# A decoder layer with experts: a sorted token list from one-hot products, adds per block, norm passes moved, one branch at the end

## Chip, cores and metric

The kernel runs on one core of a Trainium2 chip. The metric is device time in microseconds (us) of one execution. The median of three runs of the kernel before is 1720.96 us (1716.74 to 1729.13).

## What is computed

One layer of a decoder on 2048 tokens of width 1024, in float32. A mixer (windowed attention, a gated recurrence, attention into memory) and its output projection come first, then a layer norm, then a mixture of 16 experts of which each token takes two, then a second layer norm. The change lies in the expert part and in the second norm. Cut to that, the reference is:

```python
def moe(x, w_router, router_bias, w_gate, w_up, w_down):
    idx, w = route(x2, w_router, router_bias)        # two experts and weights per token
    ...                                              # assignments sorted by expert, in blocks
    def expert_block(args):
        xb, e = args
        h = jax.nn.silu(xb @ w_gate[e]) * (xb @ w_up[e])   # 1024 -> 512
        return h @ w_down[e]                                # 512 -> 1024
    ys = lax.map(expert_block, (xs, block_expert)).reshape(cap, D)
    y = jnp.zeros((n_tok, D), x.dtype).at[slot_tok].add(ys * slot_w[:, None])
    return y.reshape(B, S, D)

x = layer_norm(ALPHA * x + mix @ w_out[l], ln1_g[l], ln1_b[l])
x = layer_norm(ALPHA * x + moe(x, ...), ln2_g[l], ln2_b[l])
```

## The kernel before

The expert part begins at about 960 us of the span. `plan_slots` orders the experts by load into 16 slots s = 0 to 15, and slot s has a capacity of CAPS[s] rows, from 336 down to 256. For each slot the kernel runs `gemm1` (rows times gate and up weights, in four column blocks j; products of high and low parts, so 192 matmuls), which leaves h in a high and a low part (`L1599`, `L1600`, and `L1602` for the rows beyond a full block), and then `gemm2` (h times the down weights, by blocks of at most 128 rows, 12 matmuls for each half of the columns). The transposes of the next slot's rows (`L1484` on TensorE, `L1486` on ScalarE and VectorE) are interleaved with `gemm2`. Weights arrive over SyncE's queue, a SyncE transfer for each; ScalarE makes the high part (`L1583`, `L1560`) and VectorE the low part (`L1584`, `L1561`). `fetch` loads a small table of a slot's token numbers and weights (`tab`, also SyncE's queue), VectorE turns it into indices (`L1463`), and POOL gathers the rows of x1 (`L1471`).

Each block's result z goes to DRAM with an indirect DMA that adds into c.z (`L1673`, POOL). The DRAM tensor is one object to the dependency tracker, so each such add waits for the one before to land. c.z starts as the output of the first norm.

Tokens whose two slots are both done can have their second norm while later slots run. For that `plan_order` sorts all tokens by the later of their two slots, in six steps (`next(order_)`), spread over s = 3 to 7. It computes each token's place in the list on VectorE and scatters the token numbers to their places in DRAM, 16 indirect DMAs on POOL (`L1343`) in s = 6, and loads the list back (`L1347`) in s = 7. READY says how many blocks of 128 tokens of this list are complete after each slot: 2, 3, 5, 6, 8, 10, 12 after s = 7 to 13; the last four are taken up after s = 14. From s = 8 on `bring` gathers such blocks from c.z (`L1524`, POOL; three buffers, tile zt) and in the following slot `norm` does them: `scale` (statistics `L1531`, `L1533`, `L1535` on VectorE, a power on POOL, `L1536`) and `write` (two passes over 1024 columns, `L1541` and `L1542`, on VectorE, and an indirect write to the output, `L1546`, on POOL). With `issue_after` the VectorE work of block n is put behind the multiply of column block n (scale) and n + 1 (write) of `gemm1`, at most the fourth. In the last slot these four follow, and its own two blocks get their norm in `gemm2` itself (`normed`, `L1501` to `L1515`, with 832 columns on VectorE and the rest on ScalarE and POOL; writes `L1678`).

TensorE's order is that of the program text. The other engines' orders come from a scheduler that lays the instructions out with estimated times when the kernel is built. At the end stand two loops whose number of turns is read at run time: the first (`L1754`) does blocks over capacity, the second (`L1762`) norms all rows again where the list was not ready. With these inputs both have zero turns. `If` and loop blocks are scheduled as a unit on all engines.

## Time and profile before

| | us |
|---|---|
| median of 3 runs | 1720.96 |
| the profiled execution's own time | 1723.19 |
| its span, first to last instruction | 1721.7 |
| TensorE busy | 1544.5 (90%) |
| VectorE busy | 1199.9 (70%) |
| ScalarE busy | 755.7 (44%) |
| POOL busy | 600.5 (35%) |
| mean granted TensorE clock | 0.957 of full |
| moved by DMA | 260.77 MB, 151 GB/s over the span |

A share of busy time is an average over stages that have different limits. For the expert part one reads the windows from slot to slot: how long each is, how much of it TensorE is busy, and which wait stands in what is left. Idle time of an engine that is not the bound costs nothing. A wait for several semaphores is put down to the one that came last by the profile; where the engine named had long been done, it was another, often a DMA.

### The profile page before, as it was taken

How to read it: one execution, taken by the hardware profiler on the slowest of the kernel's cores; microseconds unless marked ns; L12 is line 12 of the kernel's file. 1: busy time of each engine (PE TensorE's matmuls, PEld its weight loads, DVE VectorE, ACT ScalarE, POOL GpSimd, SP SyncE). 2: the span in 40 equal slices, each digit the busy share in tenths (PEclk: the TensorE clock that was granted, in tenths of full speed). 3: DMA queues.
4: the chain of work that ended last, by engine and by line, in shares of the span. 5: the costliest groups of instructions: out<-in, count | busy, mean ns of one | idle time of the engine just before them, and what ended most of it. 6: DMA issues, size and time to landing. Idle time of an engine off the chain costs nothing. (4 is left out here: it accounts for less than half of the span.)

```text
span 1721.7 us, 28673 instructions
## 1 busy us (share of the span) xinstructions
PE 1544.5 (90%) x10277; PEld 1377.6 (80%) x10277; DVE 1199.9 (70%) x2900; ACT 755.7 (44%) x1589; POOL 600.5 (35%) x798
## 2 busy tenths in 40 slices
PE   8899999878899989879999599999999889998991
PEld 7899999877888888667777489998887778888881
DVE  5688888994988888768888546655555445665664
ACT  4566676764122212233332344555554445444430
POOL 3233333465554554322332222111123323242243
PEclk9999999998999999889999799999999999999996
DMA  9422222342122112263441598777767668898853
GB/s 275 140 93 93 93 93 93 129 129 82 50 63 69 56 55 93 71 223 114 158 159 74 181 266 206 203 202 199 198 185 175 168 177 231 246 271 228 236 163 117
DMA packets 241166, 260.77 MB, mean 151 GB/s; under 512 B 25301, under 2 KB 190358, under 8 KB 241020
## 3 DMA queue, kind: packets, MB, share of 16 engines
q1 hardware_dynamic: 213680, 182.11, 34.6%
q0 software_dynamic: 22224, 71.84, 15.7%
q10 hardware_dynamic: 5116, 4.94, 0.9%
q8 instruction: 83, 1.36, 0.3%
q14 instruction: 63, 0.52, 0.1%
HBM read 189.97 MB, written 70.60 MB: 151 GB/s over the span
## 5 line engine op out<-in xcount | busy, mean ns | idle before, releaser
L62 PE MATMUL ph<-xt,w 128*128 128x256 f32 (+8 forms) x3072 | 402.0, 292 | 10.0 <-ACT w L1583 3.8
L62 PEld LDWEIGHTS ph<-xt,w 128*128 128x128 f32 x3072 | 398.7, 190 | 14.7 <-DVE w L1584 5.0
L62 PE MATMUL pj<-xt,w 128*128 128x256 f32 x2016 | 293.8, 290 | 13.1 <-DVE xt L138 3.9
L62 PEld LDWEIGHTS pj<-xt,w 128*128 128x128 f32 x2016 | 262.6, 193 | 19.4 <-DVE xt L138 5.3
L1636 PE MATMUL py<-w,h 128*128 128x512 f32 (+8 forms) x936 | 253.1, 416 | 23.4 <-DVE h L1600 17.7
L1636 PEld LDWEIGHTS py<-w,h 128*128 128x128 f32 (+8 forms) x936 | 165.7, 185 | 72.7 <-DVE h L1600 21.6
L1584 DVE TENSOR_TENSOR w<-raw,w 128x1024 fp32r<-128x1024 f32 x128 | 153.7, 1218 | 67.8 <-ACT w L1583 67.6
L62 PE MATMUL py<-w,xt 128*128 128x512 f32 x672 | 172.7, 405 | 0.0
L1583 ACT ACTIVATE w<-raw 128x1024 fp32r<-128x1024 f32 x128 | 132.6, 1054 | 60.4 <-PE ph L62 34.0
L1673 POOL DMA_INDIRECT zd<-z,io x40 | 65.9, 1646 | 262.6 <-ACT xt L1486 147.0
L62 PEld LDWEIGHTS py<-w,xt 128*128 128x128 f32 x672 | 123.0, 191 | 27.1 <-issue 4.6
L1486 DVE TENSOR_TENSOR xt<-tr,xt 128x512 fp32r<-128x512 f32 (+8 forms) x84 | 49.4, 595 | 71.2 <-ACT xt L1486 71.0
L62 PE MATMUL pj<-w,xt 128*128 128x512 f32 x336 | 89.3, 405 | 0.0
L793 DVE TENSOR_TENSOR qb<-qq,F 64x256 f32<-64x256 f32 x112 | 83.4, 745 | 2.0
L338 POOL TENSOR_SCALAR prob<-prob,den 128x128 f32<-128x128 f32 x128 | 45.8, 376 | 107.7 <-ACT prob L381 57.8
L1486 ACT ACTIVATE xt<-tr 128x512 fp32r<-128x512 f32 (+8 forms) x84 | 43.7, 520 | 74.4 <-PE tr L1484 74.4
L1471 POOL DMA_INDIRECT xg<-x1d,ig x42 | 45.0, 1072 | 86.9 <-ACT w L1560 31.5
L811 DVE COPY_PREDICATED A<-mask,pl 128x512 f32<-128x512 uint8 x56 | 50.1, 894 | 34.5 <-PE pl L809 33.6
L1561 DVE TENSOR_TENSOR w<-raw,w 128x2048 fp32r<-128x2048 f32 x32 | 73.1, 2285 | 1.4 <-ACT w L1560 1.4
L1235 POOL DMA_INDIRECT T<-row,dst x32 | 34.6, 1082 | 110.9 <-DVE dst L1233 92.0
L1651 ACT ACTIVATE z<-py,tb 128x512 f32<-128x512 f32 (+1 forms) x62 | 42.6, 688 | 61.2 <-PE py L1636 59.7
L62 PEld LDWEIGHTS pj<-w,xt 128*128 128x128 f32 x336 | 60.7, 191 | 10.6
(369 smaller groups left out, 2861.6 us busy)
## 6 DMA issues: line engine op xcount, KB each, us to landing
raw<-in_w_gate SPq DMA_DIRECT2D x64, 512.0 KB
raw<-in_w_up SPq DMA_DIRECT2D x64, 512.0 KB
raw<-in_w_down SPq DMA_DIRECT2D x32, 1024.0 KB
xd<-xt SPq DMA_DIRECT2D x32, 512.0 KB
xr<-in_x SPq DMA_DIRECT2D x14, 1024.0 KB
xt<-xd POOLq DMA_DIRECT2D x20, 512.0 KB
raw<-mixT SPq DMA_DIRECT2D x16, 512.0 KB
x1d<-x SPq DMA_DIRECT2D x16, 512.0 KB
```

What stands on the lines that cost most here:

```text
L62: nc.tensor.matmul(ps, lhsT=a, rhs=b, start=i == 0, stop=i == len(steps) - 1)
L338: nc.gpsimd.tensor_scalar(prob[:, h], prob[:, h], den[:, h:h + 1], 1.0, op0=OP.mult, op1=OP.mult)
L793: nc.vector.tensor_tensor(out=qb[l][rw, :, :, o].rearrange("p a c (n i) -> p (a c) n i", i=h), in0=sec(Qv), in1=sec(Fv), op=OP.mult)
L811: c.level = nc.vector.copy_predicated(A.rearrange("p c h (n u i) -> p (c h n) u i", u=2, i=h)[:, :, 1], mask[:, l].rearrange("p m (n i) -> ...
L1471: gather = nc.gpsimd.indirect_dma_start(out=X[:r, n], out_offset=None, in_=c.x1[:, :], in_offset=indirect(ig[:r, n:n + 1]))
L1486: f["last"] = nc.scalar.activation(hi, pt, AF.Copy), v.tensor_tensor(out=lo, in0=pt, in1=f32(hi), op=OP.subtract)
L1561: v.tensor_tensor(out=t[:, 1], in0=raw, in1=f32(t[:, 0]), op=OP.subtract)
L1583: nc.scalar.activation(t[:, 0], raw, AF.Copy)
L1584: v.tensor_tensor(out=t[:, 1], in0=raw, in1=f32(t[:, 0]), op=OP.subtract)
L1636: nc.tensor.matmul(pys[hf][:m], lhsT=lhs, rhs=rhs, start=k == 0 and i == 0, stop=k == 3 and i == len(steps[k]) - 1)
L1651: nc.scalar.activation(z[:r, hs], py[:r], AF.Copy, scale=weight)
L1673: nc.gpsimd.indirect_dma_start(out=c.z[:, :], out_offset=at, in_=z[:r], in_offset=None, bounds_check=S - 1, oob_is_err=False, compute_op=O ...
```

## The change

In `plan_order` the 16 scatters and the load are replaced. The place of a token becomes a column (place divided by 128) and a row (the rest); one-hot tiles of both are built on VectorE in the buffers of tile zt (128x16x128 and 128x16x2x16, bfloat16), 16 matmuls multiply them on TensorE, and ScalarE and VectorE turn the product into the list c.fin. There are seven steps now, over s = 3 to 8. The adds into c.z go through NCH = 3 disjoint views of it, one for each block of an expert; an add waits for all adds of the expert before (`hold`) but not for those of its own. `norm` places the scale and write of block n behind the multiplies of column blocks 0 and 1 and then behind the last low part of h; in the last slot all four further blocks stand behind that low part, and their `write` puts 384 of the 1024 columns on ScalarE and POOL. At the end one branch on c.nagain holds both loops.

```diff
@@ -1287,7 +1288,7 @@
     return r
 
 
-def plan_order(c, pl, ps, r, big):
+def plan_order(c, pl, ps, yp, r, big):
 
     nc, v, cp = c.nc, c.nc.vector, c.cp
     tt = lambda o, x, y, op: v.tensor_tensor(out=o, in0=x, in1=y, op=op)
@@ -1333,18 +1334,35 @@
     yield
     tt(base, base, k[:, 0], OP.add)
     tt(base, base, hot, OP.mult)
-    dst = T([NB], "tdst", I32)
-    place = T([NB], "tplace")
+    place, col, row = T([NB], "tplace"), T([NB], "tcol"), T([NB], "trow")
     v.tensor_reduce(out=place, in_=base, axis=AX.X, op=OP.add)
-    v.tensor_copy(dst, place)
-    tok = T([NB, 2], "ttok", I32)
-    nc.gpsimd.iota(tok, pattern=[[128, NB], [0, 2]], base=0, channel_multiplier=1)
+
+    iota = T([128], "tiota", BF16)
+    nc.gpsimd.iota(iota, pattern=[[1, 128]], base=0, channel_multiplier=0, allow_small_or_imprecise_dtypes=True)
+    me = T([1], "tme")
+    nc.gpsimd.iota(me, pattern=[[0, 1]], base=0, channel_multiplier=1, allow_small_or_imprecise_dtypes=True)
+    ends = T([NB], "tends")
+    nc.gpsimd.iota(ends, pattern=[[128, NB]], base=128, channel_multiplier=0, allow_small_or_imprecise_dtypes=True)
+    ge = T([NB, NB], "m")
+    tt(ge, at(place, NB), of(ends, NB), OP.is_ge)
+    v.tensor_reduce(out=col, in_=ge, axis=AX.X, op=OP.add)
+    v.scalar_tensor_tensor(row, col, -128.0, place, op0=OP.mult, op1=OP.add)
+    yield
+
+    rows = yp.tile([128, NB, 128], BF16, name="zt", bufs=3)
+    tt(rows, iota[:, None, :].to_broadcast([128, NB, 128]), row[:, :, None].to_broadcast([128, NB, 128]), OP.is_equal)
+    cols = yp.tile([128, NB, 2, NB], BF16, name="zt", bufs=3)
+    tt(ge, of(c.iota16, NB), at(col, NB), OP.is_equal)
+    tt(cols[:, :, 0], ge, at(c.iota16, NB), OP.mult)
+    v.tensor_scalar(cols[:, :, 1], ge, me, None, op0=OP.mult)
+    yield
+    pf = ps.tile([128, 512], F32, name="py")[:, :2 * NB]
     for b in range(NB):
-        nc.gpsimd.indirect_dma_start(out=c.order[:, :], out_offset=bass.IndirectOffsetOnAxis(ap=dst[:, b:b + 1], axis=0),
-                                     in_=tok[:, b], in_offset=None)
-    yield
-    c.fin = cp.tile([128, NB, 2], I32, name="fin")
-    nc.gpsimd.dma_start(c.fin, c.order.rearrange("(b p) w -> p b w", p=128))
+        nc.tensor.matmul(pf, lhsT=rows[:, b], rhs=cols[:, b].rearrange("p a b -> p (a b)"), start=b == 0, stop=b == NB - 1)
+    fin = T([2 * NB], "tfin")
+    nc.scalar.activation(fin, pf, AF.Copy)
+    c.fin = cp.tile([128, NB], I32, name="fin")
+    v.scalar_tensor_tensor(c.fin, fin[:, :NB], 128.0, fin[:, NB:], op0=OP.mult, op1=OP.add)
     yield
 
 
@@ -1450,6 +1468,8 @@
         wg, wu, wd = a["w_gate"][0], a["w_up"][0], a["w_down"][0]
         out = a["out"][0]
 
+        zv = dram_disjoint_views(c.z[:, :], NCH)
+
         def indirect(idx):
             return bass.IndirectOffsetOnAxis(ap=idx, axis=0)
 
@@ -1535,11 +1555,18 @@
             v.tensor_scalar(t["rs"], t["mv"][:, 1:2], 1e-5 / ALPHA ** 2, None, op0=OP.add)
             nc.gpsimd.tensor_tensor(out=t["rs"], in0=t["rs"], in1=mh, op=OP.pow)
 
-        def write(t):
+        def write(t, cut=D):
 
             o = yp.tile([128, D], F32, name="o")
-            v.scalar_tensor_tensor(o, t["z"], t["mv"][:, 0:1], g2, op0=OP.subtract, op1=OP.mult)
-            v.scalar_tensor_tensor(o, o, t["rs"], b2, op0=OP.mult, op1=OP.add)
+            z, vs, ps_ = t["z"], slice(0, cut), slice(cut, D)
+            if cut < D:
+                nm = sm.tile([128, 1], F32, name="nm")
+                v.scalar_tensor_tensor(nm, t["mv"][:, 0:1], -1.0, t["rs"], op0=OP.mult, op1=OP.mult)
+                nc.scalar.activation(o[:, ps_], z[:, ps_], AF.Identity, scale=t["rs"], bias=nm)
+                nc.gpsimd.tensor_tensor(out=o[:, ps_], in0=o[:, ps_], in1=g2[:, ps_], op=OP.mult)
+                nc.gpsimd.tensor_tensor(out=o[:, ps_], in0=o[:, ps_], in1=b2[:, ps_], op=OP.add)
+            v.scalar_tensor_tensor(o[:, vs], z[:, vs], t["mv"][:, 0:1], g2[:, vs], op0=OP.subtract, op1=OP.mult)
+            v.scalar_tensor_tensor(o[:, vs], o[:, vs], t["rs"], b2[:, vs], op0=OP.mult, op1=OP.add)
             if t["idx"] is None:
                 nc.gpsimd.dma_start(out[ds(t["row"], 128), :], o)
             else:
@@ -1597,7 +1624,7 @@
                         if part < 2:
                             f["w"] = f.get("w", []) + [down(e, part)]
                 nc.scalar.activation(h[0][:, j], sl, AF.Copy)
-                low = v.tensor_tensor(out=h[1][:, j, :full], in0=sl[:, :full], in1=f32(h[0][:, j, :full]), op=OP.subtract)
+                low = f["low"] = v.tensor_tensor(out=h[1][:, j, :full], in0=sl[:, :full], in1=f32(h[0][:, j, :full]), op=OP.subtract)
                 if off:
                     v.tensor_tensor(out=ht[:, j, full + off:C + off], in0=sl[:, full:], in1=f32(h[0][:, j, full:]), op=OP.subtract)
                 if 2 in THEN[j] and late:
@@ -1606,7 +1633,7 @@
                         residual(f, C)
             f["h"] = h
 
-        def gemm2(f, e, C, late=False, last=False):
+        def gemm2(f, e, C, late=False, last=False, sums=()):
             nch = (C + 127) // 128
             h, X, off = f["h"], f["X"], stacked(C)
             W = f["w"]
@@ -1670,8 +1697,12 @@
                             yield
                 at = indirect(f["io"][:r, n:n + 1])
                 if not late:
-                    nc.gpsimd.indirect_dma_start(out=c.z[:, :], out_offset=at, in_=z[:r], in_offset=None,
-                                                 bounds_check=S - 1, oob_is_err=False, compute_op=OP.add)
+                    add = nc.gpsimd.indirect_dma_start(out=zv[n], out_offset=at, in_=z[:r], in_offset=None,
+                                                       bounds_check=S - 1, oob_is_err=False, compute_op=OP.add)
+                    for i, other in enumerate(sums):
+                        if i != n:
+                            hold(c, add, other)
+                    f["sums"] = f.get("sums", []) + [add]
                 else:
                     o = normed(z, st, r, OCUT[nch - 1 - n] if last else 0)
                     for rows_, to in (((o, out), (z, c.z[:, :])) if last else ((z, c.z[:, :]), (o, out))):
@@ -1700,7 +1731,7 @@
             r = plan_slots(c, pl, ps_y)
 
             big = lambda n: yp.tile([128, D], F32, name="zt", bufs=3)[:, :n * NE].rearrange("p (n e) -> p n e", e=NE)
-            order_, over = plan_order(c, pl, ps_y, r, big), plan_over(c, pl, r, big)
+            order_, over = plan_order(c, pl, ps_y, yp, r, big), plan_over(c, pl, r, big)
             f = start(0)
             early = sm.tile([128, 128], BF16, name="early")
             nc.scalar.activation(early, f["tb"][:, 0, 0:1].to_broadcast([128, 128]), AF.Copy)
@@ -1708,7 +1739,7 @@
             for step in transposes(f, CAPS[0]):
                 step()
                 keep_warm(c, ps_y, WARM5)
-            brought = []
+            brought, sums = [], ()
             for s in range(NE):
                 late = last = s == NE - 1
                 nxt = start(s + 1) if 0 < s < NE - 1 else None
@@ -1723,46 +1754,51 @@
                         after(order, f["mul"])
                         for _ in range(15):
                             next(over, None)
-                        for _ in range(0 if s < 3 else 2 if s == 5 else 1):
+                        for _ in range(0 if s < 3 else 2 if s == 4 else 1):
                             next(order_, None)
-                def norm(n, t):
-
-                    for k, part in enumerate((scale, write)):
-                        with ExitStack() as order:
-                            after(order, f["muls"][min(n + k, 3)])
-                            part(t)
-
-
-                ids = [c.fin[:, b, 0:1] for b in range(READY[s - 2] if s > 1 else 0, READY[s - 1] if s else 0)]
+                def norm(n, t, cut=D):
+
+                    marks = f["muls"][:2] + [f["low"]]
+                    with ExitStack() as order:
+                        after(order, marks[min(n, 2)])
+                        scale(t)
+                    with ExitStack() as order:
+                        after(order, marks[min(n + 1, 2)])
+                        write(t, cut)
+
+
+                ids = [c.fin[:, b:b + 1] for b in range(READY[s - 2] if s > 1 else 0, READY[s - 1] if s else 0)]
                 for n, t in enumerate(brought):
                     norm(n, t)
                 brought = [bring(idx=i) for i in ids[:3]]
                 if last:
                     for n in range(len(ids)):
-                        norm(2 + n // 2, brought[n])
+                        norm(2, brought[n], 640)
                         if n + 3 < len(ids):
                             brought.append(bring(idx=ids[n + 3]))
-                work = gemm2(f, E[s], CAPS[s], late, last)
+                work = gemm2(f, E[s], CAPS[s], late, last, sums)
                 if nxt:
                     steps = transposes(nxt, CAPS[s + 1])
                     interleave(work, [(0.8 * (k + 0.5) / len(steps), f) for k, f in enumerate(steps)])
                 else:
                     run(work)
+                sums = f.get("sums")
                 f = nxt
 
-        n = nc.values_load(c.nover[0:1, 0:1], min_val=0, max_val=NOV)
-        with tc.For_i(0, n, 1) as i:
-            e = nc.sync.value_load(c.oexp[0:1, ds(i, 1)], min_val=0, max_val=NE - 1)
-            row = nc.sync.value_load(c.orow[0:1, ds(i, 1)], min_val=0, max_val=NE * EROWS - 128)
-            f = fetch(row, 128)
-            run(transposes(f, 128))
-            gemm1(f, e, 128)
-            run(gemm2(f, e, 128))
-        n = nc.values_load(c.nagain[0:1, 0:1], min_val=0, max_val=S // 128)
-        with tc.For_i(0, n, 1) as i:
-            t = bring(row=i * 128)
-            scale(t)
-            write(t)
+        again = nc.values_load(c.nagain[0:1, 0:1], min_val=0, max_val=S // 128)
+        with tc.If(again > 0):
+            n = nc.values_load(c.nover[0:1, 0:1], min_val=0, max_val=NOV)
+            with tc.For_i(0, n, 1) as i:
+                e = nc.sync.value_load(c.oexp[0:1, ds(i, 1)], min_val=0, max_val=NE - 1)
+                row = nc.sync.value_load(c.orow[0:1, ds(i, 1)], min_val=0, max_val=NE * EROWS - 128)
+                f = fetch(row, 128)
+                run(transposes(f, 128))
+                gemm1(f, e, 128)
+                run(gemm2(f, e, 128))
+            with tc.For_i(0, S // 128, 1) as i:
+                t = bring(row=i * 128)
+                scale(t)
+                write(t)
 
 
 def fill_tables(c, pad, part):
```

## Rows read from the trace of the kernel before

**Rows 1.** Windows from gemm2 to gemm2: length; busy us (count) by engine; clock; DMA; GB/s.

```profile
1190.50:1233.10 42.60, 42.60 (x285) 37.99 (x284) 25.28 (x56) 22.91 (x33) 7.37 (x6) 1.00 0.75 197
...
1277.20:1321.70 44.50, 42.68 (x282) 37.26 (x282) 19.64 (x30) 19.55 (x28) 17.44 (x14) 1.00 0.68 159
1321.70:1373.20 51.50, 45.00 (x282) 38.61 (x281) 23.19 (x37) 24.76 (x36) 15.38 (x13) 0.93 0.74 188
1373.20:1422.00 48.80, 43.86 (x283) 37.12 (x282) 24.42 (x40) 22.38 (x32) 10.00 (x9) 0.93 0.70 195
...
1464.60:1506.10 41.50, 37.69 (x259) 34.55 (x258) 26.59 (x36) 19.32 (x26) 10.27 (x8) 0.96 0.86 241
1506.10:1546.40 40.30, 37.55 (x257) 34.48 (x257) 26.18 (x35) 19.32 (x26) 14.55 (x10) 0.96 0.94 267
...
1629.10:1669.80 40.70, 37.58 (x257) 34.40 (x256) 26.54 (x35) 17.18 (x25) 14.90 (x10) 0.96 0.72 204
```

**Rows 2.** Waits, 1255 to 1400 us: who, for whom; total us, times, longest.

```profile
POOL ord L1343 <- DMA ord<-ttok,tdst: 52.3, 14, 7.2
...
DVE tb L1463 <- DMA tab<-T: 23.1, 3, 10.4
ACT z L1651 <- DMA zd<-z,io: 21.5, 2, 12.0
```

**Rows 3.** Timeline, 1348 to 1393 us: start, length, engine, line; idle before, releaser.

```profile
1348.43 1.65 POOL L1673 DMA_INDIRECT zd<-z,io  x1 [0.30 <-issue]
1354.72 0.72 ACT L1651 ACTIVATE z<-ys,tb 16x512 f32<-16x512 f32 x1 [11.97 <-DMA zd<-z,io]
...
1358.94 0.51 PE L62 MATMUL ph<-xt,w 128*128 128x264 f32 x2 [3.33 <-ACT w L1583]
...
1392.44 0.59 PE L1484 MATMUL tr<-ident,xg 8*128 8x8 f32 x4 [4.69 <-DVE xt L1486]
```

**Rows 4.** Waits, 1400 to 1670 us.

```profile
DVE tb L1463 <- DMA tab<-T: 26.5, 4, 8.6
...
PE py L1636 <- DVE h L1600: 15.1, 6, 3.4
...
DVE o L1542 <- POOL rs L1536: 2.5, 1, 2.5
```

**Rows 5.** Timeline, 1500 to 1516 us, expert 11.

```profile
1508.01 1.27 DVE L1541 SCALAR_TENSOR_TENSOR o<-zt,mv,g 128x1024 f32<-128x1024 f32 x1
...
1510.34 0.41 DVE L1600 TENSOR_TENSOR h<-sl,h 128x256 fp32r<-128x256 f32 x1
...
1510.80 0.63 PE L1636 MATMUL py<-w,h 128*128 128x512 f32 x1 [2.75 <-DVE h L1600]
```

**Rows 6.** Chain that ended last (start, length, what): loop at the end.

```profile
1703.52 0.04 DVEq L1754
```

**Rows 7.** Timeline, 1704 to 1709 us, last norms.

```profile
1704.68 0.59 POOL L1511 TENSOR_TENSOR o<-o,b 128x192 f32<-128x192 f32 x1 [2.35 <-issue]
1704.77 1.38 DVE L1515 SCALAR_TENSOR_TENSOR o<-o,rs,b 128x832 f32<-128x832 f32 x1 [4.49 <-issue]
...
1707.25 1.08 DVE L1515 SCALAR_TENSOR_TENSOR o<-o,rs,b 128x832 f32<-128x832 f32 x1
```

**Rows 8.** Groups from 1000 us: line, engine, names, shapes, count; busy, mean ns; idle.

```profile
L1561 DVE TENSOR_TENSOR w<-raw,w 128x2048 fp32r<-128x2048 f32 x31 | 70.9, 2286 | 1.4 <-ACT w L1560 1.4
...
L1308 PEld LDWEIGHTS <-tri 128*128 128x128 bf16 x1 | 0.1, 96 | 0.1
```

**Rows 9.** Timeline on POOL, 1440 to 1470 us, expert 9's blocks.

```profile
1445.31 1.61 POOL L1673 DMA_INDIRECT zd<-z,io  x1 [0.31 <-ACT ys L1645]
1454.00 3.35 POOL L1673 DMA_INDIRECT zd<-z,io  x1 [7.09 <-ACT w L1583]
```

**Rows 10.** Timeline on TensorE, 1629 to 1722 us, the last gemm2.

```profile
1673.61 3.06 PE L1636 MATMUL py<-w,h 128*128 128x512 f32 x12 [1.68 <-DVE h L1600]
```

**Rows 11.** Groups on POOL, whole span, forms kept apart.

```profile
L1162 POOL TENSOR_TENSOR x<-x,g 128x384 f32<-128x384 f32 x15 | 15.3, 1022 | 37.8 <-ACT x L1161 20.0 <-ACT sc L1174 17.5
```

More of the change, by code (lines that the diff above doesn't have):

```diff
@@ L8 @@
 from concourse import mybir
+from concourse.ap import dram_disjoint_views
 from concourse.bass import ds
@@ L1786, in build @@
         c.z = c.dram.tile([S, D], F32, name="zd")
-        c.order = c.dram.tile([S, 2], I32, name="ord")
         c.T = [c.dram.tile([NE * EROWS, 2], F32, name=f"T{j}") for j in range(2)]
```

## The prediction

> **What bounds the kernel now.** I read the windows by expert first, then the waits of two stretches, then the timeline where a wait was long, and last the end of the span. Expert numbers count the sixteen slots s = 0 to 15; a window runs from one expert's second product (gemm2) to the next one's, so it holds gemm2(s) and gemm1(s+1). In the window of s = 4 [rows 1] TensorE is busy 42.6 of 42.6 us: that is what an expert costs when nothing is late, and later experts have fewer rows. So between experts the path is TensorE, and only its holes can be won there. The reader is to see three kinds of hole.
>
> First, s = 6 to 8: the windows take 44.5, 51.5 and 48.8 us [rows 1]. The waits of that stretch [rows 2] say why: POOL stood 52.3 us on the scatters of the order list, each of which waits for the one before to land. POOL is in order, so the accumulating scatters of expert results stand behind them. One issues only at 1348.4, ScalarE has by then waited 12.0 us for the buffer that it reads, and TensorE has 3.3 us without split weights [rows 3]. Second, s = 9 to 14: TensorE waits six times, 15.1 us in all, for the low part of h (L1600) [rows 4]. In s = 11 VectorE does the 1.27 us pass L1541 of a norm, and then a weight split, before the low part that the ninth matmul of gemm2 needs; the hole is 2.75 us [rows 5]. Four of the six are like it, about 2.7 us; the longest, in s = 10, is 3.4 [rows 4], and what is left, 0.9, is s = 12. Five windows, the first and last of which are shown, also have a granted clock of 0.96 [rows 1]: at the half level for 8% of some 41 us, 1.6 us lost in each. Third, the end. At 1703.5 the chain that ended last runs through a loop of zero turns (L1754), in the middle of the last norms [rows 6], and VectorE stands 4.49 us [rows 7]. TensorE has long finished; VectorE's and POOL's work sets the end there.
>
> **The sorted list.** Sixteen scatters, the load of the list and a wait for each go. Of the three windows, the excess over 42.6 us is 1.9, 8.9 and 6.2 us, 17.0 together. I take back about two thirds of the first, 1.2 (the rest is a wait on transposes), all of the second, whose holes lead to that one queue, and half of the third: its largest hole, 4.69 us [rows 3], is VectorE standing up to 10.4 us for a table load (L1463) [rows 2], which may be weights catching up after the late scatters or may be there anyway. That is 13.2. Added on TensorE's own path are 16 small matmuls at expert 8; a weight load of that shape took 96 ns [rows 8], so 1.6 us. On VectorE the one-hot rows are 128x2048: the nearest row is 2.29 us [rows 8]; three passes on 256 columns come on top. They sit in s = 7, where VectorE is busy 23.2 of 51.5 us [rows 1] and no norm pass runs yet; that slack hides them, and if they land ahead of a low part instead they cost up to their 2.3 us once. Three iotas on POOL replace the scatters; I count them as nothing, since POOL is idle there once the chain is gone. Sum of this part: 13.2 - 1.6 = 11.6. Bounds: 1.8 (half of the second window, nothing of the third, one-hot rows on the path) and 15.4 (all three windows, less the matmuls).
>
> **Adds side by side.** An expert's second add now waits for the previous expert's adds, long landed, not for its own first. At 1454.0 such an add issues 8.7 us after its neighbour [rows 9]; behind it on POOL stand the gathers of finished rows and the small power op of the norm, for which VectorE then stands 2.5 us [rows 4]. This is the s = 10 hole of 3.4 us: without the stand 0.9 is left. Elsewhere the adds free POOL earlier and no row shows that TensorE would gain; zero there. Nothing new queues behind them: the holds name adds that have landed a whole expert before.
>
> **Norm passes behind h's last rows.** With two blocks, the second block's write moves from behind the third product's multiply to behind the last low part. That takes L1541, 1.3 us [rows 5], out of the four holes of 2.7 us (s = 9, 11, 13, 14), leaving 1.4 each. The first block's passes and the second's statistics stay where they are, so the hole does not vanish; s = 12 has one block and keeps its 0.9. Of 15.1 us 7.4 stay (four times 1.4, 0.9 and 0.9) and 7.7 go. After a hole of 1.68 us twelve matmuls took 3.06 us [rows 10], 512 columns each at 2.4 GHz, so holes of 1.4 should not drop the clock: four windows get 1.6 us back, 6.4 (in the fifth the drop follows a wait on transposes). Against it: gemm2 comes earlier, but the table load stands behind weights, and the DMA share is already 0.94 in one window [rows 1]. I give back 4 for that. This part with the one before: 7.7 + 6.4 - 4 = 10.1, bounds 0 and 23.1 (all holes and all five clock losses).
>
> **The end.** The new branch writes the output, so it cannot stand before the last norms as the first loop does: 4.49 us go. Of the last four finished blocks 384 of 1024 columns move to ScalarE and POOL: 1.27 us becomes about 0.8, eight times, 3.8 us off VectorE. POOL does 128x384 in 1.02 us [rows 11], and it is not free: L1515 took 1.38 us beside POOL's L1511 and 1.08 nearly alone [rows 7]. In proportion eight such ops cost VectorE 0.5 each, 4.2; as only some meet a two-input op I take half, 2.1. Sum: 4.5 + 3.8 - 2.1 = 6.2. The one branch that is left I price like the last loop, nothing won; if it needs no reset at all, a stand like the 4.5 us of the first goes too. Bounds 0.1 (below) and 12.8.
>
> The Trainium skill, SBUF — State Buffer, section Who interferes with whom, says that a VectorE instruction with two SBUF inputs and a GpSimd instruction that reads SBUF exclude each other for the whole instruction. The 0.30 us above agrees in sign and is half of POOL's 0.59 us. By the rule at its fullest the end would give 0.1 instead of 6.2; the case stands among the rivals. The Trainium skill, DMA: Bandwidth & Descriptors, section Issuing engines are not separate DMA queues, says that all issuers share the same 16 engines; by it adds in parallel bring no bandwidth, and in the worst case the 2.5 us of s = 10 stays and the sum is 25.4; no run here shows two of these adds at once.
>
> **Sum.** 11.6 + 10.1 + 6.2 = 27.9. The profiled span of 1721.7 becomes 1693.8; 1.5 us lie outside the span, so 1695.3 against 1723.19. The median of the runs shown is 2.2 lower than that profiled run, so 1693.
>
> **The rivals.**
> *All holes close (0.15).* VectorE, no longer late, has every low part ready, and the stand on the table was only catch-up: 15.4 + 23.1 + 8.3 (the end without POOL's toll) = 46.8, so 1674. For it: the window of s = 4 has no hole at all [rows 1]. Against it: the first block's passes stay ahead of the low parts.
> *The transfers take over (0.17).* Weights and tables set the pace from s = 8 on, so part two wins nothing and the half of the third window neither: 8.5 + 6.2 = 14.7, so 1706. For it: the 0.94 share and the 23.1 us of table waits [rows 1, 2]. Against it: the other windows from s = 8 to 14 lie at 0.86 or below, so there is room for two or three us each.
> *POOL holds VectorE at the end (0.10).* Each of eight POOL ops blocks VectorE for its whole 1.02 us, 8.2 us: the end gives 4.5 + 3.8 - 8.2 = 0.1, so 1699. For it: the stretched L1515. Against it: it was stretched by half of the POOL op only, and half of VectorE's tail work is statistics or reads PSUM. The rule of the Trainium skill on SBUF, above, speaks for it too.
> *Slower (0.05).* The adds in one burst lie on the DMA engines just when the tables and the weights of the next expert are asked for, and every expert pays the 4.69 us that only s = 8 pays now: 13 more times 4.69 is 61, so 1754. It cancels the gain from six experts on and ends over 1% slower from ten. For it: the stand at L1463 is already there [rows 2]. Against it: the bytes are the same, and in s = 9 to 14 four table waits, 26.5 us together [rows 4], cost TensorE far less than that.
> That the adds stay serial after all, through the holds, would move only the 2.5 us of s = 10; it is within the forecast.
>
> **How the numbers follow.** The forecast has 0.53, with a range of its own of 1680 to 1704. Faster by over 1% (under 1703.8; about what a measurement of this kernel tells from no change) are the forecast, the first and the third rival: 0.78. Within 1% is the second, 0.17; slower by over 1% the fourth, 0.05. For 8 in 10 the range reaches down to the first rival and up past the second, leaving out the slow case and about half of the first: 1674 to 1710.
>
> **What would show it.** Right: no wait of ScalarE for z on a scatter in s = 6 to 8, and windows there of 42 to 46 us; two adds of an expert within 2 to 4 us of each other on POOL where their data allow; waits on h's low part of about 7 us in all in s = 9 to 14, and a granted clock of 1.00 in most windows; no reset of semaphores between the last norms, and POOL's two-tensor ops of 1.0 us beside VectorE passes of 0.8 to 1.3. Wrong: the instruction order is laid out anew from estimated times, so a norm's write can land before a table's transposes and stop TensorE there; a DMA share over 0.95 with waits of the weight splits on raw loads; or a last norm that ends later than about 1702 on the old clock, less what was won before.

## The result, and the profile after

The changed kernel takes 1702.65 us, median of five runs (1699.13 to 1709.15); the ratio to the kernel before is 0.9895, interval 0.9858 to 0.9932. Measured again, the same kernel took 1701.82 us, 0.9883 [0.9855, 0.9912]. The profiled execution took 1709.15 us, the slowest of its five, with a span of 1707.5, against 1721.7 before. I cut each span at three places: the start of gemm2 for s = 0, for s = 9, and for s = 15.

| us | until s=0 | s=0 to 9 | s=9 to 15 | s=15 to end | span |
|---|---|---|---|---|---|
| before | 1011.6 | 410.4 | 247.9 | 51.8 | 1721.7 |
| after | 1008.2 | 398.3 | 249.2 | 51.8 | 1707.5 |
| after, again | 1004.9 | 394.5 | 249.7 | 51.9 | 1701.0 |

So by these stretches the whole gain lies ahead of s = 9. The expert part starts 3.4 and 6.7 us earlier than before although no code ahead of it was changed, so this is taken as scatter; of the 6.5 us between the two profiles of after it makes 3.3. The stretch from s = 15 to the end took 51.5 to 51.9 us in four profiles of kernels whose end is that of after, and 52.9 in a fifth; below about 1.5 us nothing is read from it alone.

Windows from gemm2 to gemm2 of after, which answer to [rows 1]: s = 4, 6, 7, 8, then s = 10, 11, 13 and 14. Columns as there.

```profile
1188.80:1231.20 42.40, 42.40 (x283) 37.80 (x282) 25.91 (x57) 22.92 (x33) 7.39 (x6) 1.00 0.72 197
...
1274.90:1316.70 41.80, 41.80 (x283) 37.13 (x282) 24.96 (x38) 22.28 (x32) 7.44 (x6) 1.00 0.74 201
1316.70:1359.20 42.50, 41.26 (x298) 36.39 (x297) 22.01 (x34) 22.41 (x33) 6.50 (x5) 1.00 0.70 196
1359.20:1406.50 47.30, 43.65 (x287) 36.98 (x284) 23.97 (x40) 22.20 (x33) 11.10 (x10) 0.93 0.69 194
...
1448.50:1493.50 45.00, 39.70 (x259) 36.00 (x257) 24.41 (x35) 20.67 (x28) 7.99 (x8) 0.92 0.77 218
1493.50:1537.70 44.20, 38.38 (x259) 35.55 (x258) 26.27 (x35) 19.20 (x26) 14.45 (x10) 0.92 0.85 243
...
1579.60:1617.70 38.10, 36.18 (x259) 33.35 (x258) 26.62 (x35) 19.22 (x27) 9.43 (x8) 1.00 0.86 247
1617.70:1655.70 38.00, 36.08 (x259) 33.27 (x257) 26.53 (x36) 17.05 (x25) 13.37 (x11) 1.00 0.77 225
```

The holes of s = 6 and 7 are closed, but for 1.2 us in s = 7. s = 8 keeps its own. s = 13 and 14 are 2.6 us (it was 40.7) and 2.7 us shorter, at a granted clock of 1.00, and s = 10 and 11 are 3.5 to 4 us longer than [rows 1] shows for them, at a granted clock of 0.92. Waits of after for s = 9 to 14 (1386 to 1656 us), against [rows 4]:

```profile
DVE tb L1483 <- DMA tab<-T: 32.9, 4, 9.3
...
PE ph L63 <- DVE xt L1506: 9.5, 4, 4.3
...
PE py L1663 <- DVE h L1627: 7.5, 6, 1.5
```

The waits for h's low part are halved, from 15.1 to 7.5. In their place TensorE waits 9.5 us for xt's low part; before, it was 2.8 in this stretch. The timeline of expert 11 shows how (against [rows 5]):

```profile
1497.03 0.50 PE L1663 MATMUL py<-w,h 128*128 128x512 f32 x1 [1.53 <-DVE h L1627]
...
1498.71 1.27 DVE L1568 SCALAR_TENSOR_TENSOR o<-zt,mv,g 128x1024 f32<-128x1024 f32 x1
...
1501.29 4.96 SPq L1481 DMA_DIRECT2D tab<-T  x2
...
1513.07 0.16 DVE L1483 TENSOR_TENSOR tb<-tab 128x4 f32<-128x4 f32 x1 [9.23 <-DMA tab<-T]
...
1513.42 0.69 DVE L1506 TENSOR_TENSOR xt<-tr,xt 128x512 fp32r<-128x512 f32 x1
...
1514.16 6.04 PE L63 MATMUL ph<-xt,w 128*128 128x256 f32 x30 [4.29 <-DVE xt L1506]
```

The norm pass L1568 now stands behind h, and the hole there is 1.53, as forecast. But VectorE then stands 9.23 us at L1483 for the next table of tokens, which SP asked for at 1501.29, behind weights; a split of xt that gemm1 needs is queued behind L1483, and TensorE pays 4.29 us. The last of these stands ends at 1555 us, in s = 12; s = 13 and 14 have none, and of these six windows they are the two that became clearly shorter.

s = 10 has, beside its wait for xt, a hole of another kind (timeline):

```profile
1451.11 1.06 ACT L1610 ACTIVATE w<-raw 128x1024 fp32r<-128x1024 f32 x1 [4.88 <-DMA raw<-in_w_gate]
...
1452.53 0.73 PE L1663 MATMUL py<-w,h 128*128 128x512 f32 x2 [2.48 <-ACT h L1626]
```

ScalarE stands 4.88 us for gate weights, and the high part of h behind them is late. In the second profile of after it stands 2.86 us for up weights there, and TensorE waits 2.10 us for the low part.

### The profile page after: what moved, and what is told of

Read it like the earlier page. It is cut to its first block, busy times and chain, and to the rows that moved or that the text cites. A ratio compares the mean times of both kernels' runs of the same rounds, so it can differ in the third digit from the quotient of the medians.

```text
span 1707.5 us, 28568 instructions
## 1 busy us (share of the span) xinstructions
PE 1535.2 (90%) x10293; PEld 1372.7 (80%) x10293; DVE 1203.9 (71%) x2911; ACT 758.9 (44%) x1594; POOL 580.7 (34%) x791
## 5 line engine op out<-in xcount | busy, mean ns | idle before, releaser
L63 PEld LDWEIGHTS ph<-xt,w 128*128 128x128 f32 x3072 | 400.2, 191 | 16.9 <-DVE xt L1506 12.1
L1663 PE MATMUL py<-w,h 128*128 128x512 f32 (+8 forms) x936 | 244.2, 406 | 11.4 <-DVE h L1627 7.5
L1663 PEld LDWEIGHTS py<-w,h 128*128 128x128 f32 (+8 forms) x936 | 160.3, 179 | 58.0 <-DVE h L1627 10.1
L1700 POOL DMA_INDIRECT zd<-z,io x40 | 62.3, 1557 | 306.5 <-ACT xt L1506 207.4
L1616 ACT ACTIVATE sl<-ph 128x256 f32<-128x256 f32 (+8 forms) x64 | 25.8, 403 | 113.3 <-PE ph L63 113.2
```

The source lines that it names most:

```text
L63: nc.tensor.matmul(ps, lhsT=a, rhs=b, start=i == 0, stop=i == len(steps) - 1)
L1663: nc.tensor.matmul(pys[hf][:m], lhsT=lhs, rhs=rhs, start=k == 0 and i == 0, stop=k == 3 and i == len(steps[k]) - 1)
L1700: add = nc.gpsimd.indirect_dma_start(out=zv[n], out_offset=at, in_=z[:r], in_offset=None, bounds_check=S - 1, oob_is_err=False, compute_op ...
```

## The experiments

Two theories went in. **Table:** the token table's place, in SP's queue and in VectorE's line, took back what part two (the adds and the norm passes) won. **Transfers:** the DMA engines themselves set the pace from s = 8 on, so nothing asked for elsewhere would help. Ratios are to the kernel before on the same chip, from all runs and so not the quotient of two medians, with a 95% interval; the stretches come from one profiled execution each.

| kernel | median us | ratio | s=0 to 9 | s=9 to 15 | s=15 to end |
|---|---|---|---|---|---|
| list alone | 1709.46 | 0.9945 [0.9924, 0.9965] | 389.9 | 252.2 | 53.6 |
| old marks | 1711.55 | 0.9906 [0.9874, 0.9937] | 393.4 | 254.7 | 54.5 |
| adds chained | 1703.00 | 0.9860 [0.9826, 0.9894] | 393.5 | 249.9 | 51.9 |
| two loops | 1704.67 | 0.9921 [0.9894, 0.9947] | 390.4 | 251.5 | 56.0 |
| no cut | 1702.84 | 0.9903 [0.9876, 0.9930] | 392.5 | 249.8 | 50.4 |
| output views | 1698.94 | 0.9859 [0.9822, 0.9896] | 396.8 | 246.6 | 48.7 |
| early table | 1679.57 | 0.9747 [0.9714, 0.9780] | 388.3 | 232.0 | 51.5 |
| before + early table | 1726.40 | 1.0028 [1.0006, 1.0049] | 425.0 | 243.1 | 52.0 |
| early table, old marks | 1688.93 | 0.9819 [0.9785, 0.9852] | 388.4 | 239.4 | 54.7 |
| early table, adds chained | 1698.26 | 0.9866 [0.9832, 0.9899] | 402.8 | 235.8 | 52.9 |
| early table, views, no cut | 1674.70 | 0.9736 [0.9703, 0.9768] | 388.3 | 231.2 | 46.3 |

### The changed kernel again

No edit.

> The changed kernel once more, as the yardstick for the runs beside it. Both theories: 0.989 of the kernel before, about 1703 us; gemm2 of s = 9 starts some 15 us earlier than before, and from there to the last instruction nothing is won (51.8 us from the last gemm2 to the end in both profiles).

It repeats the first result; the table above the experiments has its stretches.

### The sorted list alone

The kernel before with the new `plan_order`, and nothing else of the change:

```diff
-    c.fin = cp.tile([128, NB, 2], I32, name="fin")
-    nc.gpsimd.dma_start(c.fin, c.order.rearrange("(b p) w -> p b w", p=128))
+    for b in range(NB):
+        nc.tensor.matmul(pf, lhsT=rows[:, b], rhs=..., start=b == 0, stop=b == NB - 1)
...
```

> The kernel before with the sorted list from one-hot products alone. Theory A (the list is what pays): 11 to 14 us faster than before, 0.992 to 0.994; gemm2 of s = 9 starts 11 to 14 us earlier, waits on h's low part stay near 15 us and the last norms keep the loop in their middle. Theory B (the parts need one another, the list alone only moves the wait to the chain of adds): under 5 us, 0.997 or more.

The ratio gives 9.5 us, with the interval 6.0 to 13.1: short of the 11 to 14 of the first theory, and over the 5 of the second. (Its profiled execution, 1700.40 us, is the fastest of twelve and lies 9 us below their median, so its stretches may be short.) Its windows of s = 7 and 8:

```profile
1309.20:1350.40 41.20, 41.20 (x297) 36.40 (x296) 22.04 (x34) 22.34 (x33) 6.47 (x5) 1.00 0.75 208
1350.40:1393.20 42.80, 41.29 (x289) 36.18 (x286) 24.05 (x40) 22.23 (x33) 11.68 (x10) 1.00 0.78 212
```

No hole is left in s = 7, so the scatters were its whole excess. In s = 8 this execution shows 42.8 us and after shows 47.3 with the same list, but s = 9 takes 47.7 us here and 42.0 in after: VectorE stands 10.05 us for a table at 1411.66, so the hole has moved one window on, across the line at which the stretches are divided.

### Old marks, and adds in one chain

Each undoes half of part two in the changed kernel.

```diff
-                    marks = f["muls"][:2] + [f["low"]]
-                        after(order, marks[min(n, 2)])
+                    marks = f["muls"]
+                        after(order, marks[min(n, 3)])
...
-        zv = dram_disjoint_views(c.z[:, :], NCH)
+        zv = [c.z[:, :]] * NCH
```

(The first four lines are the one kernel, the last two the other; in the first the last norms also go back to `2 + n // 2`.)

> The changed kernel with the norm passes behind the multiplies as before, in the last slot too. Theory A: TensorE's waits on h's low part from s = 9 to 15 go from 7.5 back to 13 to 15 us, its waits on the transposes fall by some 3 us because the table has more time, and the stretch from s = 9 to s = 15 is 2 to 4 us longer than 249. Theory B (the marks decide nothing): both waits and the stretch as in the changed kernel.

> The changed kernel with the adds into z one behind the other again. Theory A: the second add of a slot issues 6 to 9 us after the first; VectorE stands about 2.5 us for the power op in s = 10 and TensorE's wait there is 2 to 3 us longer; the whole within 3 us of the changed kernel. Theory B (adds side by side are what makes slots s = 5 to 8 short): the stretch from s = 0 to s = 9 is 5 us or more longer than 390 to 398.

With the old marks TensorE waits 12.7 us for h from s = 9 to 15, against 7.5 and 9.0 in the two profiles of after, and the stretch is 5 us longer. Part of that is the table's hole, which here lies in s = 9 (49.3 us): counted from s = 8 the stretch is 1.3 and 3.4 us longer. The waits on the transposes did not fall (10.4 us, against 9.5 and 11.4), and the end is 2.7 us longer. Chaining the adds leaves every stretch within 1 us of the second profile of after, but for one hole at s = 10. POOL of the chained kernel in s = 9, then its TensorE in s = 10:

```profile
1424.46 1.62 POOL L1700 DMA_INDIRECT zd<-z,io  x1 [0.30 <-issue]
1435.04 2.01 POOL L1700 DMA_INDIRECT zd<-z,io  x1 [8.96 <-DMA zd<-z,io]
```

```profile
1448.89 0.75 PE L1663 MATMUL py<-w,h 128*128 128x512 f32 x1 [3.80 <-DVE h L1627]
```

The same two adds in after, POOL:

```profile
1429.84 1.62 POOL L1700 DMA_INDIRECT zd<-z,io  x1 [0.30 <-issue]
1431.77 1.36 POOL L1700 DMA_INDIRECT zd<-z,io  x1 [0.30 <-issue]
```

The adds do go side by side, 1.9 us apart in place of 10.6, and the hole of 3.80 us is the one forecast from [rows 9]. It is 1.3 to 1.7 us longer than the 2.48 and 2.10 of after, as the weights come late there, and no ratio shows it. Read alone, these two runs say that part two is worth 5 us at most. The runs with the early table say otherwise.

### The table one slot earlier

The changed kernel, with `fetch`'s two table loads taken out into `table()`. Slot s's start uses the table asked for a slot earlier and asks for that of s+1, on the same queue.

```diff
+            f = fetch(E[s] * EROWS, CAPS[s], TB.get(s))
+            if 0 < s < NE - 1:
+                E[s + 1] = nc.sync.value_load(c.eslot[0:1, s + 1:s + 2], ...)
+                TB[s + 1] = table(E[s + 1] * EROWS, CAPS[s + 1])
+            return f
```

> The changed kernel with each slot's small token table asked for one slot earlier on the same queue; bytes and everything else as they are. Theory A (what the shorter holes won is lost again because VectorE stands at the table, and with it the low parts of the next slot's transposes): TensorE's waits on those low parts from s = 9 to 15 fall from 10 to 13 us to under 4, the stretch from gemm2 of s = 9 to that of s = 15 from 249 to about 240 us, the whole 7 to 11 us faster than the changed kernel, about 0.983 of before. Theory B (the transfers as a whole set the pace there): the waits turn into waits of the weight splits on their loads, the stretch stays within 3 us of 249.

From s = 9 to 15 the span falls by 17 us, about twice what was expected, and no wait of TensorE for xt is left from s = 0 on. Windows of s = 8, 10 and 11, against after's above:

```profile
1352.30:1393.80 41.50, 41.33 (x287) 36.26 (x284) 23.95 (x40) 22.25 (x33) 11.14 (x10) 1.00 0.79 223
...
1434.90:1472.30 37.40, 36.12 (x259) 33.31 (x258) 23.88 (x35) 19.32 (x26) 11.47 (x8) 1.00 0.86 247
1472.30:1513.50 41.20, 37.68 (x259) 34.87 (x258) 27.12 (x36) 19.32 (x26) 14.46 (x10) 0.96 0.89 267
```

s = 10 takes 37.4 us in place of 45.0, at a clock of 1.00 in place of 0.92. The same bytes go through the same engines, and faster: 247 GB/s against 218. So the transfers theory falls, and the table theory stands for the changed kernel.

VectorE's stand at the table does not vanish: it falls from 82.0 us in 13 waits to 28.3 in three, two of them from s = 9 on. In the trace VectorE uses each table one slot earlier too, and where it still stands, no split of xt is behind it (VectorE in s = 11):

```profile
1485.12 0.69 DVE L1512 TENSOR_TENSOR xt<-tr,xt 128x512 fp32r<-128x512 f32 x1 [2.53 <-ACT xt L1512]
1496.52 0.19 DVE L1489 TENSOR_TENSOR tb<-tab 128x4 f32<-128x4 f32 x1 [10.71 <-DMA tab<-T]
```

What is left there is a wait of 2.02 us for a weight split. The table loads still stand behind weights in SP's queue. Whether the earlier load wins by itself, or the new order on VectorE, no run separates.

### The early table in the kernel before

> The kernel before with one edit: the token table of slot s+1 is asked for on SP's queue right behind slot s's weights, one slot earlier; scatters, chained adds, norm passes and the two loops stay as they were. Theory 1 (the table only became the limit once the norm passes had moved): before waited 7.6 us (first nine slots) and 2.8 us (s=9 to 15) of TensorE for xt's low half behind the table, so these two sums go and little else: first stretch 410 to about 402, s=9 to 15 248 to about 244, h waits near 15 as before, median about 1711, ratio .993. Rival (the table set part two's pace before too, and the moved passes are worth nothing): s=9 to 15 falls to 232 to 235 as with the change, ratio .985 or lower. The scatters, 52 us on POOL in slots 6 to 8, should still be there in both.

Both theories missed: it gains nothing, it loses 0.06 to 0.49%. s = 9 to 15 is shorter by 4.8 us, as the first theory had it, but s = 0 to 9 is longer by 14.6. TensorE's waits for h fall to 11.0 us, where 15 were expected. VectorE's waits from 1010 to 1660 us, of before and then of this kernel:

```profile
DVE tb L1463 <- DMA tab<-T: 77.2, 13, 10.4
```

```profile
DVE tb L1469 <- DMA tab<-T: 13.3, 2, 7.8
```

```profile
DVE io L1473 <- DMA zd<-z,io: 66.4, 12, 10.1
```

The table is waited for twice only. Four lines on, `fetch` casts the table's indices into io, and there VectorE now stands for an add to c.z to land, nearly as long. In before the same line (L1467) never stood for a DMA; why is said with the next pair of runs. Where the adds stand on POOL behind the list's scatters it is worst (window of s = 6, 60.7 us):

```profile
1323.79 1.44 POOL L1679 DMA_INDIRECT zd<-z,io  x1 [0.86 <-DMA zd<-z,io]
```

```profile
1327.74 0.21 DVE L1473 CAST io<-tb 128x2 int32<-128x2 f32 x1 [10.08 <-DMA zd<-z,io]
```

```profile
1328.44 0.79 PE L62 MATMUL ph<-xt,w 128*128 128x272 f32 x2 [5.74 <-DVE sl L1596]
```

### The early table with half of part two undone

> The changed kernel with the early table, but all of an expert's accumulating adds in one chain. Theory (the side-by-side adds buy only s=10's hole): s=9 to 15 at 232 to 234, ratio .974 to .977. Rival (with the table gone the chain of adds is the next to be late, 7 us each, and weights' buffers or z tiles come free later): s=9 to 15 at 238 or more, ratio .979 or higher.

The rival holds by the ratio: with the adds in a chain the early table wins nothing (0.9866, and 0.9860 with the late one), and against 0.9747 the difference, 0.0119 of 1721.76, is 20 us. It does not hold by place: s = 9 to 15 stays under its 238, and 14.5 us are lost from s = 0 to 9. And what waits first is not weights or z tiles, but VectorE at the cast in `fetch`. VectorE's wait at the cast, chained and then side by side:

```profile
DVE io L1493 <- DMA zd<-z,io: 56.6, 11, 7.0
```

```profile
DVE io L1493 <- DMA zd<-z,io: 13.6, 10, 3.7
```

One turn of it in the chained kernel: the last add of an expert issues, and VectorE stands until it has landed 7 us later.

```profile
1080.75 1.63 POOL L1706 DMA_INDIRECT zd<-z,io  x1 [1.48 <-DMA zd<-z,io]
```

```profile
1087.89 0.17 DVE L1493 CAST io<-tb 128x3 int32<-128x3 f32 x1 [6.87 <-DMA zd<-z,io]
```

Side by side the last add issues at once, so it lands before the cast is due or soon after. The pool that holds io has four buffers, and that is why the cast waits for so recent an add: the cast at 1087.89 is the sixth of 16, that of slot 5, though it runs in the window of s = 1, and the buffer it takes was slot 1's, whose last add is the one at 1080.75. With the table late VectorE runs `fetch` three slots ahead (the last of 16 casts falls in s = 12), and the buffer belongs to an expert whose adds have landed long before; the early table makes it four (s = 11). More buffers were not tried.

> The changed kernel with the early table, but the norm passes at their old marks. Theory (with the table out of the way the moved marks are worth what h's waits cost): TensorE's waits for h in s=9 to 15 rise from 6.9 to 12.5 or more and s=9 to 15 from 232.0 to 238 to 241, the tail from 51.5 to about 54; ratio about .980. Rival (the marks are worth nothing; the table was all of it): s=9 to 15 at 232 to 233, ratio .974 to .975.

The theory holds: 0.9819 against 0.9747 is 0.0072, 12 us. TensorE's wait for h (1392 to 1640 us) is back near the 15.1 of [rows 4], 13.1 without the seventh wait, which lies in s = 15:

```profile
PE py L1669 <- DVE h L1633: 14.8, 7, 2.8
```

So the two halves of part two are worth 20 and 12 us once the table is early, and 0 to 5 when it is late. Of the 12, 7.4 lie from s = 9 to 15 and 3.2 in the end.

### The end: two loops, no cut, separate output views

```diff
-        again = nc.values_load(c.nagain[0:1, 0:1], ...)
-        with tc.If(again > 0):
+        n = nc.values_load(c.nover[0:1, 0:1], ...)
+        with tc.For_i(0, n, 1) as i:
...
-                        norm(2, brought[n], 640)
+                        norm(2, brought[n])
...
-                nc.gpsimd.indirect_dma_start(out=out, out_offset=..., in_=o, in_offset=None)
+                wrote.append(nc.gpsimd.indirect_dma_start(out=ov[len(wrote) % 2], out_offset=..., in_=o, in_offset=None))
```

Three kernels, each the changed one with one of these. In the third the last expert's rows have views of their own, held behind the last four writes.

> The changed kernel with the two loops at the end as before, in place of the branch. Theory A (the loop in the middle of the last norms costs what VectorE stood there, 4.5 us): 3 to 6 us slower, the last gemm2 to the end 55 to 58 us. Theory B (POOL's chain of output writes hides it): within 2 us, 51 to 53 us.

> The changed kernel with the 384 columns of the last slot's four blocks back on VectorE. Theory A (POOL's queue with its output writes sets the end): the same or up to 4 us faster, the stretch from the last gemm2 to the end 48 to 52 us. Theory B (VectorE's work sets the end, as the prediction had it): 2 to 4 us slower, 54 to 56 us.

> The changed kernel with the output writes of finished blocks alternating between two disjoint views of the output, the last slot's own blocks on two more (held behind the last four), and z of the last slot on the adds' views. Theory A (the writes landing one behind the other on POOL's queue set the end): from the last gemm2 to the end 44 to 48 us instead of 51.8. Theory B (POOL's and VectorE's own work sets it): 50 to 52 us.

Two loops make the end 4.2 us longer (56.0 against 51.8). The stand of [rows 7] is back; VectorE of that kernel:

```profile
1683.52 1.38 DVE L1535 SCALAR_TENSOR_TENSOR o<-o,rs,b 128x832 f32<-128x832 f32 x1 [4.41 <-issue]
```

Taking the cut away makes the end 1.4 us shorter, at the edge of what can be read, and moves the total by less than its interval: the 384 columns on POOL win nothing that can be seen. VectorE and POOL of after:

```profile
1670.11 0.98 POOL L1567 TENSOR_TENSOR o<-o,b 128x384 f32<-128x384 f32 x1
1670.16 1.90 DVE L1564 SCALAR_TENSOR_TENSOR nm<-mv,rs 128x1 f32<-128x1 f32 x1
...
1671.05 0.98 POOL L1566 TENSOR_TENSOR o<-o,g 128x384 f32<-128x384 f32 x1
...
1677.62 1.49 DVE L1569 SCALAR_TENSOR_TENSOR o<-o,rs,b 128x640 f32<-128x640 f32 x1
```

A VectorE pass on one column, 0.15 us elsewhere, lasts 1.90, until both POOL passes beside it are done. What ends last in after is then a row of output writes, each landing before the next (chain that ended last), for which VectorE stands, as o has two buffers (timeline):

```profile
1683.33 3.42 DMA out<-o,fin
1687.54 3.56 DMA out<-o,fin
...
1691.90 3.60 DMA out<-o,io
```

```profile
1686.77 1.08 DVE L1534 SCALAR_TENSOR_TENSOR o<-z,mv,g 128x832 f32<-128x832 f32 x1 [3.23 <-DMA out<-o,fin]
...
1691.19 1.08 DVE L1534 SCALAR_TENSOR_TENSOR o<-z,mv,g 128x832 f32<-128x832 f32 x1 [2.22 <-DMA out<-o,fin]
```

With separate views the end is 3.1 us shorter, between the bounds of the two theories, and these two stands are 2.39 and 0.93 us.

### A faster kernel

The early table, the output views and no cut together.

> The changed kernel with the early table, the separate views of the output at the end, and the last list norms whole on VectorE (no 640 cut). Theory (the three gains lie in different stretches and add): s=9 to 15 at 232, tail 51.8 - 3.1 - 1.4 = 47 to 48, median 1679.6 - 4 = about 1675, ratio .970 to .973. Rival (with the writes no longer in a chain, VectorE is late at the end, so taking the 384 columns back onto it costs): tail 50 or more, ratio .975 or higher.

The end is 46.3 us, 5.2 less than with the early table alone. The total, 1674.70 us and 0.9736, is the lowest measured, by the ratios 25 to 27 us under the changed kernel; its lead over the early table alone (0.9747) lies inside the intervals.

## Why the prediction was right or wrong

The time lies in the range (1674 to 1710), 10 us above the forecast. By the stretches two of its three sums failed and the first held, so the place in the range is not to the credit of the mechanism: the range was wide enough for a rival in which part two wins nothing.

The two ways of counting do not quite agree. By the ratios the list alone is worth 9.5 us and the rest of the change 9 to 11 (0.9945 against 0.9895 and 0.9883); the stretches from s = 9 on give that rest nothing. As the list's only profile is its fastest execution, where the rest lies is not shown.

**Sorted list, 11.6: right.** Alone it gives 9.5 [6.0, 13.1]; s = 0 to 9 fell by 12.1 and 15.9 in the two profiles of after. The second window gave all of its excess, as reckoned. The 16 matmuls were oversized, 1.6 against 0.6, and the one-hot rows took 2.28 us, hidden: they run in the window of s = 6, which has no hole. Groups of after:

```profile
L1294 DVE TENSOR_TENSOR zt<-tiota,trow 128x2048 bf16<-128x2048 bf16 x1 | 2.3, 2284 | 0.0
...
L1361 PE MATMUL py<-zt 128*128 128x32 bf16 x16 | 0.6, 177 | 0.0
L1361 PEld LDWEIGHTS <-zt 128*128 128x128 bf16 x16 | 0.5, 96 | 0.0
```

The third window stayed at 47.3 us (44.7 in the second profile). Half of its excess was to go; its hole was the table's, not catching up: the scatters are gone, and VectorE stands 8.9 us for a table there.

**Adds and norm passes, 10.1: wrong.** The waits for h came out at 7.5 (9.0 in the second profile) where 7.4 was forecast, though not in their places: s = 10 was to keep 0.9, and keeps 2.48 behind late weights. The step that failed is the 4 us given back to the table, and with it the 6.4 of the clock. Waits for xt rose by 6.7 (2.8 to 9.5), a wait for h's high part on ScalarE added 2.5, and the clock returned nothing on the whole: s = 13 and 14, which have no table to wait for, came out at 1.00 with holes of 1.5 us, as reckoned, but two windows at 0.92 and one at 0.96 lose 45.0 x 0.08 + 44.2 x 0.08 + 41.9 x 0.04 = 8.8 us, where the five windows at 0.96 lost 8.2 before. The stretch went from 247.9 to 249.2. The row that gave it away was at hand: in [rows 4] VectorE waits 26.5 us for tables. I took it as harmless since TensorE waited little then. The stand grew to 32.9 us as the waits for h shrank: what shortens VectorE's way to L1463 lengthens its stand there.

The rival in which the transfers take over named this outcome (part two wins nothing, 1706), and 1702.65 lies nearer to it than to the forecast. Its reason holds for the late weights of s = 10 at most: the early table moves no fewer bytes and wins 17 us in that stretch. Of the 2.5 us given for the adds at s = 10, 1.3 to 1.7 came (3.80 chained, 2.48 and 2.10 side by side), and the sentence that the adds win nothing elsewhere holds only while the table is late.

**The end, 6.2: wrong.** The loop's 4.5 was right (4.2). The cut, 3.8 less 2.1, was to win 1.7 and wins nothing, or costs 1.4 by the stretch. The rival in which POOL holds VectorE has the mechanism, and the 1.90 us pass above shows it: two whole POOL passes, not the half that I took from [rows 7]. Four VectorE passes beside the 384-column ones are longer than their like by 1.75, 0.61, 0.80 and 0.21 us, 3.4 in all where 2.1 was taken off, so that little of the 3.8 is left. In the 1.90 us pass the trace agrees with the Trainium skill, SBUF — State Buffer, section Who interferes with whom, that the two exclude each other for the whole instruction. What remains isn't settled. The loop's 4.2 and the 2.7 us that the moved marks are worth in the end, less 1.4 for the cut, should have shown 5.5 us, and the stretch is as long as before. With the list alone and the old end it is already 1.8 us longer than before; what the scheduler laid out differently there was not followed. The output writes in a row, which I did not cost at all, end last (3.1 us by the views).

## What to carry to other kernels

Ahead of moving work off an in-order engine, list what that engine waits for next and how long it has stood there so far: a stand that costs nothing today is where the gain goes. When an edit measures nothing, undo it again with the next wait taken away, since one edit can put work at a place where only the other keeps it from waiting: the adds were worth 0 and then 20 us, and the early table -5 us alone and about 24 with the change. Where an in-order engine stands for a small load, ask for it a stage earlier, and see which buffers the engine then reaches for; a place ahead of the large loads in the queue was not tried here.

## What was not expected of the hardware

- A VectorE pass over one column lasted 1.90 us beside two POOL passes of 0.98.
- Sixteen bfloat16 products with 32 columns, each with its own weight load, took 0.6 us of TensorE together.
- An indirect write of one block of output landed in 3.4 to 3.6 us, and in a row these, not the arithmetic, ended the kernel.
